# Two layers of a pooling and attention trunk: VectorE instead of GpSimd adds the two branches, and the sums of weights are all made in the first layer

## The chip, the cores and the metric

The kernel runs on one core of a Trainium2 chip. The metric is the time of one execution on the device in microseconds (us). The core's engines run side by side, each through its own queue in order: TensorE (PE, with its weight loads shown as PEld) multiplies matrices, VectorE (DVE), ScalarE (ACT) and GpSimd (POOL) work element by element, and SyncE (SP) starts transfers (DMAs). Engines wait for each other through semaphores. GpSimd starts transfers too.

## The reference, cut to what matters

The model width is 1024, there are 512 tokens and 16 meta tokens ahead of them (528 in all), and two layers. Everything is float32. Per layer:

```
h = rmsnorm(h_res, norm_gain[l])
u_pool, z_pool, c_q, c_kv, k_rope, z_mla, g_pool, g_mla = split(h @ w_in[l])
y_pool = (pool_mix(u_pool, pool_w_group[l], pool_scale[l]) * silu(z_pool)) @ pool_w_up[l]
o_mla  = mla(c_q, c_kv, k_rope, ...)            # 8 heads, causal, low-rank q and kv, QK-norm, rotary
y_mla  = (o_mla * silu(z_mla)) @ mla_w_up[l]
merged = sigmoid(g_pool) * y_pool + sigmoid(g_mla) * y_mla
h_res  = h_res + merged @ w_out[l]
```

`pool_mix` takes causal means over windows of 2, 4, 8 and 16 tokens in four groups of channels, subtracts the token itself and multiplies by a 128x128 matrix per group. The meta tokens are dropped from the output.

## The kernel before

**Tiles.** Channels lie on the 128 partitions, tokens along the free axis. A product of 1024 channels is eight output tiles of 128 channels; each is computed from eight blocks of 128 input channels. Every float32 operand is split into a high part and a rest (`hh`/`hl` for activations, `whi`/`wlo` for weights), and one block of a product is three matmuls (`mm3`, lines 188, 191, 192): high by high, rest by high, high by rest. In the first layer an output tile is made in two segments of 264 tokens; in the last layer in one of 512, since the meta tokens are no longer needed there.

**The stream of weights.** `register` lists all products of both layers in the order in which TensorE does them: latent inputs, `u`, `zp`, `y` (the pooled branch), `qr`/`qn`, `pu` (up-projection of the pooled branch), `zm`, gates, `mu` (up-projection of the attention branch) and `o` (output). `stream` walks the list in chunks of 512 weight columns (256 KB) and has the loads four chunks ahead. `wload` starts the load into one of three buffers `raw` on SP's queue (line 115); ScalarE makes `whi` (line 183) and VectorE `wlo` (line 184), and then the `raw` buffer is free for the next load. A loop in `go` places everything else, such as the attention heads, between steps of the stream; `after(ns, fn)` has a piece of work done when the stream has gone on by a modelled time. A scheduler then sets each engine's order from a modelled timeline.

**Merging the branches (`ev_mu`, lines 1046 to 1054).** `am[m]` holds tile m of the gated pooled branch, in the buffer `xb`; `gms[m]` holds the attention gate, in a `cq` buffer. For each segment of an up-projection tile VectorE computes (gate + 1) times the matmul's result (line 1051), GpSimd adds the pooled branch (line 1052), ScalarE takes the high part `hh` (line 298), and VectorE the rest `hl` (line 299). The output products read these as `hh`/`hl` of block m. After the up-projection `blend` (lines 1086 to 1089) forms further sums of tiles on VectorE for the output products.

**Sums of weights (`weight_sums`).** Some output tiles and gates are computed in pairs with seven smaller products instead of eight, which needs sums of quarters of two weight tiles. They are made by transfers alone, in device memory (`wsum`): a copy on SP's queue (line 351), and an accumulating transfer on GpSimd's queue (line 354). A unit takes four of each; there are two units for each layer's output weights and four for the last layer's pooled gates (`gp`). Each transfer is held back until a matmul that stands some way back in the stream has been done:

```python
def copy(d, src):
    behind(sp.dma_start(d, src[0]), earlier(9000))

def add(d, src):
    behind(gp.dma_start(d, src[1], accum_op=ALU.add), earlier(4000))
```

In the first layer `go` starts them after `qn3`: 16 transfers for the first layer's output weights, one per 3500 modelled ns, then 22 of the 32 for the gates, one per 4000. The other ten are kept in the list `jobs` and placed at the start of the last layer, from `norm_sums` on. The last layer's own output weights are summed during its heads.

**Start of a layer (`norm_sums`).** The rows of inverse norms go out to memory by four small transfers (`ndr`, lines 434 and 435) and come back spread over all partitions (`rinv` and `q`, line 440), all on SP's queue, in which the weight loads stand as well.

Of the kernel before, what the change touches and what calls it, by code (L numbers as in the profile page):

```python
# [23 lines left out]
T = SEQ + NM  # L24
# [15 lines left out]
MT_GP = 16  # L40
# [18 lines left out]
OUT = (3, 4, 5, 6)  # L59
# [13 lines left out]
def trunk(ctx, tc, xT, pos, win, wkr, wqb, wkb, wvb, wgr, wpu, wmu, wout, gains, const, yT):  # L73
    nc = tc.nc
    pe, act, dve, gp, sp = nc.tensor, nc.scalar, nc.vector, nc.gpsimd, nc.sync
# [86 lines left out]
    class Gemm:  # L162
        def __init__(self, name, src, width, evac=None, xs=None, segs=None, body=None, gain=None):
            self.name, self.src, self.width, self.alloc = name, src, width, mmt
            self.evac, self.xs, self.segs, self.body, self.gain = evac, xs, segs, body, gain
            self.spare = self.more = False
# [30 lines left out]
    def earlier(ns):  # L197
        return next((m for c, m in reversed(past) if c <= clk[0] - ns), past[0][1])

    newest = [None]  # L200
    jobs = []
    plan = []
    done = set()

# [57 lines left out]
    def after(ns, fn):  # L262
        pend.append((clk[0] + ns, fn))
        pend.sort(key=lambda e: e[0])
# [9 lines left out]
    def upto(name):  # L274
        while name not in done:
            if not step():
                break
# [19 lines left out]
    def split(hi, lo, src, a, b):  # L297
        act.activation(hi[:, a:b], src, AF.Copy)  # L298
        dve.tensor_sub(lo[:, a:b], src, hi[:, a:b].bitcast(F32))  # L299

    def behind(ins, other):
        tc.add_manual_dep(ins.ins, other.ins.name,
                          mybir.DependencyInfo(mybir.DependencyClass.Sync, mybir.DependencyReason.DATA))
# [38 lines left out]
    def weight_sums(name, w):  # L342
        def made(u, i):
            a, b = w[2 * u], w[2 * u + 1]
            d = wsum[name][u]
            src = {0: (b[:, 0:512], b[:, 512:1024]), 2: (a[:, 0:512], b[:, 0:512]), 1: (a[:, 0:512], d[:, 0, :]),
                   3: (a[:, 512:1024], d[:, 1, :])}
            return d[:, i, :], src[i]
# [7 lines that stand above are left out]
        for u in range(len(w) // 2):  # L356
            for fn, i in ((copy, 0), (copy, 2), (add, 0), (copy, 1), (add, 2), (add, 1), (copy, 3), (add, 3)):
                yield lambda fn=fn, u=u, i=i: fn(*made(u, i))

    class Layer:  # L360
        def __init__(self, l):
            self.l, self.last = l, l == DEPTH - 1
            self.XS = XTOK if self.last else FULL
            self.x0 = NM if self.last else 0
            self.xt = xt if l == 0 else [None] * 8
            self.hs, self.us, self.zps = hbuf, [None] * 4, [None] * 4
            self.cs, self.cqs, self.ys, self.am = [None] * 2, [None] * 6, [None] * 4, [None] * 8
            self.kn, self.qn, self.zms, self.ogs = [None] * 4, [None] * 4, [None] * 4, [None] * 4
            self.qr, self.qf = [None] * 2, [None] * 2
            self.gms, self.mg, self.xr, self.vw = [None] * 8, [None] * 8, [None] * 8, []  # L370
            self.made = [None] * 8
            self.csq, self.xsq = [None] * 2, [None] * 8
            self.sq = []
            self.sums = [None] * 8
            self.f, self.tt, self.part = [None] * 8, [None] * 4, {}
            self.st = self.acc = self.inv = self.cinv = self.kraw = self.kp = None

# [668 lines left out]
        def ev_mu(self, m):  # L1046
            def ev(ps, a, b):
                if a == self.x0:
                    self.mg[m] = self.hs[m]
                t = self.gms[m][:, a:b]  # L1050
                dve.scalar_tensor_tensor(out=t, in0=t, scalar=1.0, in1=ps, op0=ALU.add, op1=ALU.mult)  # L1051
                self.sums[m] = gp.tensor_add(t, t, self.am[m][:, a:b])  # L1052
                split(*self.mg[m], t, a, b)
            return ev

        def ev_o(self, m, nxt):
# [187 lines left out]
        def go(self, nxt):  # L1244
            l = self.l
            up = lambda name: upto((l, name))
# [10 lines left out]
                for k in range(8):  # L1257
                    self.square_x(k)
            self.norm_sums()
            if l == 1:  # L1260
                for i in range(len(jobs)):
                    after(4000 * (i + 1), jobs.pop(0))
            up("u1")
            for m in range(2):
                self.mix(m, self.window(m))
# [6 lines left out]
            up("zp1")  # L1272
            self.mix(3, s3)
            self.k_factors()
            up("qr1")
            for s, (a, b) in enumerate(FULL):
                a0 = max(a, self.x0)
                self.stat(self.acc[:, a0:b], a0, b, C_CQ, self.acc_last)
            up("qn3")
            if l == 0:  # L1280
                jobs.extend(weight_sums("gp", [win[1, MT_GP + m] for m in range(8)]))
                for i, fn in enumerate(weight_sums(0, [wout[0, m] for m in OUT])):
                    after(3500 * (i + 1), fn)
                for i in range(22):
                    after(16 * 3500 + 4000 * (i + 1), jobs.pop(0))
            self.qk_stats()
            if l == 0:
                fill_now(2600)
# [117 lines left out]
```

## Time and profile before

| | |
|---|---|
| median of 3 runs | 793.72 us (793.56 to 794.35) |
| the profiled execution, its own time | 794.64 us |
| its span, first to last instruction | 792.8 us |
| busy share: PE, PEld, DVE, ACT, POOL | 98%, 90%, 76%, 56%, 30% |
| line 1052 on GpSimd, 24 instructions | 28.6 us |
| transfers from start to landing, median | weights (`raw<-win`) 2.8 us; copies for sums 3.5 to 4.0; accumulating ones 5.7 to 6.1 |

TensorE is busy for nearly all of the span, so its short waits are what can be won, and new waits of it are what can be lost. Where a view lists windows, it gives for each stretch its length and each engine's busy time with the number of instructions that fall in it, then the granted TensorE clock (1.00 is full), the DMA engines' busy share and GB/s. Where a view lists waits, it gives the total, the number and the longest. A name such as `mm<-hl,whi` says what is written from what, without buffer numbers; a time of a transfer is from its start on the queue to its landing.

### The profile page before, as it was taken

What the parts mean: (1) busy time and instruction counts of PE and PEld (TensorE: products, weight loads), DVE (VectorE), ACT (ScalarE), POOL (GpSimd) and SP (SyncE); (2) the same over time, 40 slices, a digit from 0 to 9 for tenths busy, and PEclk for the clock granted to TensorE, in tenths of its full rate; (3) what the DMA queues carried; (4) which work ended last, traced back from release to release, by engine and by line L of the source; (5) the groups of instructions that cost most, each with busy time, mean ns of one, the idle gap of its engine ahead of it and who ended that gap; (6) DMA issues with size and microseconds to landing.
All of it is one profiled execution on the core that took longest, in us unless ns stands there. A gap on an engine that the chain in (4) does not pass through costs nothing. (4 is left out here: it accounts for less than half of the span.)

```text
span 792.8 us, 15386 instructions
## 1 busy us (share of the span) xinstructions
PE 778.1 (98%) x5493; PEld 713.7 (90%) x5493; DVE 601.0 (76%) x1321; ACT 443.6 (56%) x1015; POOL 238.5 (30%) x315
## 2 busy tenths in 40 slices
PE   8999999999999999999999999999999999999898
PEld 8999899999999999999997887887788989988687
DVE  5848788447788887689865378775997989975985
ACT  8536656645566565545564256555657766763451
POOL 1034505013443352072100246131026335431601
PEclk9999999999999999999999999999999999999999
DMA  6242343566546546655632754435456666662552
GB/s 241 82 101 92 90 118 101 153 146 159 130 122 142 129 121 136 162 146 176 183 116 74 139 126 122 132 87 175 124 128 147 182 164 169 166 232 82 165 165 80
DMA packets 65196, 109.15 MB, mean 138 GB/s; under 512 B 10448, under 2 KB 16976, under 8 KB 65120
## 3 DMA queue, kind: packets, MB, share of 16 engines
q1 hardware_dynamic: 58096, 93.72, 40.3%
q0 software_dynamic: 6016, 12.62, 9.8%
q10 hardware_dynamic: 1008, 1.84, 0.6%
q8 instruction: 43, 0.70, 0.4%
q14 instruction: 33, 0.27, 0.1%
HBM read 100.18 MB, written 22.62 MB: 155 GB/s over the span
## 5 line engine op out<-in xcount | busy, mean ns | idle before, releaser
L188 PE MATMUL mm<-hh,whi 128*128 128x264 f32 (+2 forms) x1000 | 308.7, 311 | 2.9 <-ACT whi L183 2.8
L191 PE MATMUL mm<-hl,whi 128*128 128x264 f32 (+2 forms) x1000 | 306.9, 308 | 2.3 <-DVE hl L299 2.3
L192 PE MATMUL mm<-hh,wlo 128*128 128x264 f32 (+2 forms) x1000 | 306.4, 309 | 1.0 <-DVE wlo L184 1.0
L184 DVE TENSOR_TENSOR wlo<-raw,whi 128x512 fp32r<-128x512 f32 (+2 forms) x261 | 195.3, 752 | 100.0 <-ACT whi L183 93.6
L183 ACT ACTIVATE whi<-raw 128x512 fp32r<-128x512 f32 (+2 forms) x261 | 156.2, 602 | 142.7 <-PE mm L191 76.5
L188 PEld LDWEIGHTS mm<-hh,whi 128*128 128x128 f32 x1000 | 188.2, 189 | 14.0 <-ACT whi L183 3.5
L191 PEld LDWEIGHTS mm<-hl,whi 128*128 128x128 f32 x1000 | 188.7, 189 | 12.0 <-DVE hl L299 3.2
L192 PEld LDWEIGHTS mm<-hh,wlo 128*128 128x128 f32 x1000 | 187.8, 189 | 10.4 <-DVE wlo L184 2.1
L192 PE MATMUL mm<-cq,wlo 128*128 128x264 f32 (+2 forms) x156 | 48.0, 310 | 0.7 <-DVE wlo L184 0.7
L188 PE MATMUL mm<-cq,whi 128*128 128x264 f32 (+2 forms) x156 | 48.6, 311 | 0.0
L704 POOL TENSOR_TENSOR racc<-racc,tmp 128x264 f32<-128x264 f32 (+1 forms) x15 | 14.3, 952 | 112.2 <-ACT tmp L703 88.1
L191 PE MATMUL mm<-cq,whi 128*128 128x264 f32 (+2 forms) x140 | 43.5, 312 | 0.0
L1052 POOL TENSOR_TENSOR cq<-cq,xb 128x264 f32<-128x264 f32 (+1 forms) x24 | 28.6, 1220 | 46.8 <-DVE cq L1051 46.6
L881 DVE CUSTOM_DVE_ANT_0 S<-S,maskw,nqs 128x288 f32<-128x288 f32 (+4 forms) x80 | 38.2, 496 | 2.6 <-PE S L192 2.4
L188 PE MATMUL mm<-u,whi 128*128 128x264 f32 (+1 forms) x108 | 35.2, 326 | 0.0
L192 PE MATMUL mm<-u,wlo 128*128 128x264 f32 (+1 forms) x108 | 34.8, 322 | 0.0
L299 DVE TENSOR_TENSOR tl<-mm,th 128x512 fp32r<-128x512 f32 (+1 forms) x64 | 29.4, 480 | 7.0 <-ACT th L298 6.0
L354 POOL DMA_DIRECT2D wsum<-wout x8 | 6.8, 848 | 87.8 <-PE mm L192 82.2
L852 POOL TENSOR_TENSOR tmp<-kp,bc 64x528 f32<-64x528 f32 x16 | 24.8, 1550 | 25.8 <-DVE xb L653 9.5
L192 PEld LDWEIGHTS mm<-cq,wlo 128*128 128x128 f32 x156 | 29.4, 188 | 2.6 <-DVE wlo L184 1.1
L928 POOL TENSOR_TENSOR cq<-cq,rs 128x384 f32<-128x384 f32 (+1 forms) x32 | 31.6, 989 | 0.0
L888 ACT ACTIVATE cq<-S,bia 128x400 f32<-128x400 f32 (+2 forms) x48 | 24.5, 515 | 12.1 <-DVE bia L916 7.9
(341 smaller groups left out, 1714.6 us busy)
## 6 DMA issues: line engine op xcount, KB each, us to landing
raw<-win SPq DMA_DIRECT2D x139, 256.0 KB, 2.8
raw<-wout SPq DMA_DIRECT2D x22, 256.0 KB, 3.0
bc<-kdr SPq DMA_DIRECT2D x16, 264.0 KB, 4.6
raw<-wpu SPq DMA_DIRECT2D x16, 256.0 KB, 3.0
wsum<-wout SPq DMA_DIRECT2D x16, 256.0 KB, 3.5
wsumgp<-win SPq DMA_DIRECT2D x16, 256.0 KB, 4.0
raw<-wmu SPq DMA_DIRECT2D x16, 256.0 KB, 2.8
raw<-wsumgp SPq DMA_DIRECT2D x16, 256.0 KB, 3.4
```

What stands on the lines that cost most here:

```text
L183: act.activation(hi[:, :n], raw[:, :n], AF.Copy)
L184: dve.tensor_sub(lo[:, :n], raw[:, :n], hi[:, :n].bitcast(F32))
L188: first = pe.matmul(out, wh, xh, start=start, stop=False, skip_group_check=more)
L191: pe.matmul(out, wh, xl, start=False, stop=False, skip_group_check=more)
L192: newest[0] = pe.matmul(out, wl, xh, start=False, stop=stop, skip_group_check=more)
L299: dve.tensor_sub(lo[:, a:b], src, hi[:, a:b].bitcast(F32))
L704: self.acc_last = gp.tensor_add(self.acc[:, a:b], self.acc[:, a:b], t[:, :b - a])
L852: gp.tensor_mul(kf[r0:r0 + 64, :], self.kp[r0:r0 + 64, :], bc[r0:r0 + 64, :])
L881: dve.tensor_tensor_reduce(out=sv, in0=sv, in1=mask, scale=nqs[:, i, h:h + 1], scalar=3e38, op0=ALU.add, op1=ALU.min, accum_out=bia[:, c:c ...
L888: act.activation(pv, sv, AF.Exp, scale=-1.0, bias=bia[:, i:i + 1], accum_out=rs[:, c:c + 1])
L928: gp.tensor_mul(pt[i][:, NM:], pt[i][:, NM:], rs[:, i:i + 1].to_broadcast([P, n - NM]))
L1052: self.sums[m] = gp.tensor_add(t, t, self.am[m][:, a:b])
```

## The change

GpSimd no longer adds the pooled branch. VectorE adds it, once per tile and over all tokens, when the tile's last segment has come (in the first layer that joins two segments); the split into `hh` and `hl` is then done once over the whole tile too. The sums of weights for the first layer's output and for the last layer's gates are now all 48 started after `y3`, ahead of `qr`, in one row at 4000 modelled ns each. The list `jobs` and its use in the last layer are gone.

```diff
-    jobs = []
...
-            self.sums = [None] * 8
...
                 dve.scalar_tensor_tensor(out=t, in0=t, scalar=1.0, in1=ps, op0=ALU.add, op1=ALU.mult)
-                self.sums[m] = gp.tensor_add(t, t, self.am[m][:, a:b])
-                split(*self.mg[m], t, a, b)
+                if b == T:
+                    t, x0 = self.gms[m], self.x0
+                    dve.tensor_add(t[:, x0:T], t[:, x0:T], self.am[m][:, x0:T])
+                    split(*self.mg[m], t[:, x0:T], x0, T)
             return ev
...
-            if l == 1:
-                for i in range(len(jobs)):
-                    after(4000 * (i + 1), jobs.pop(0))
             up("u1")
...
             self.k_factors()
+            up("y3")
+            if l == 0:
+                sums = [*weight_sums(0, [wout[0, m] for m in OUT]), *weight_sums("gp", [win[1, MT_GP + m] for m in range(8)])]
+                for i, fn in enumerate(sums):
+                    after(4000 * (i + 1), fn)
             up("qr1")
...
             up("qn3")
-            if l == 0:
-                jobs.extend(weight_sums("gp", [win[1, MT_GP + m] for m in range(8)]))
-                for i, fn in enumerate(weight_sums(0, [wout[0, m] for m in OUT])):
-                    after(3500 * (i + 1), fn)
-                for i in range(22):
-                    after(16 * 3500 + 4000 * (i + 1), jobs.pop(0))
             self.qk_stats()
```

Three places show what the scheduler makes of it. In the names, `raw` is a weight buffer, `wsumgp3` a unit of sums for the gates, `ndr` the small transfers of the norms, `cq5` the tile of up-projection 5, and `mm_1946`, `mm_1971`, `mm_1981` the first three output tiles of the last layer.

SP's queue at the start of the last layer, before:

```order
L435 DMA ndr11_118<-ny2_1098_6122 16x1
L351 DMA wsumgp2_125<-win 128x512
L115 DMA raw_1140_6309<-win 128x512
L115 DMA raw_1145_6341<-wkb 128x256
L440 DMA rinv_1100_6141<-ndr10_117 128x528
L440 DMA q1_1101_6142<-ndr11_118 128x528
L115 DMA raw_1149_6375<-win 128x512
L115 DMA raw_1157_6404<-win 128x512
L351 DMA wsumgp3_126<-win 128x512
L115 DMA raw_1162_6437<-wkr 128x256
L351 DMA wsumgp3_126<-win 128x512
```

And after the change:

```order
L433 DMA ndr11_118<-ny2_1098_6108 16x1
L115 DMA raw_1140_6294<-win 128x512
L115 DMA raw_1145_6326<-wkb 128x256
L438 DMA rinv_1100_6127<-ndr10_117 128x528
L438 DMA q1_1101_6128<-ndr11_118 128x528
L115 DMA raw_1149_6359<-win 128x512
L115 DMA raw_1157_6388<-win 128x512
L115 DMA raw_1162_6420<-wkr 128x256
```

The copies have gone from this part of the queue, and the loads follow the norms directly; five copies and five accumulating transfers leave the last layer in all.

VectorE at the end of the last layer's up-projection, before:

```order
L299 TENSOR_TENSOR hl4_15_141<-cq4_1902_9653,hh4_14_140 128x512
L1051 SCALAR_TENSOR_TENSOR cq5_1903_9655<-cq5_1903_9655,mm_1934_9812 128x512
L184 TENSOR_TENSOR wlo_1992_10068<-kh_1990_10065,whi_1991_10067 128x512
L299 TENSOR_TENSOR hl6_19_145<-cq6_1887_9611,hh6_18_144 128x512
L1051 SCALAR_TENSOR_TENSOR cq7_1907_9681<-cq7_1907_9681,mm_1942_9858 128x512
L184 TENSOR_TENSOR wlo_2002_10110<-kl_2000_10107,whi_2001_10109 128x512
L299 TENSOR_TENSOR hl5_17_143<-cq5_1903_9655,hh5_16_142 128x512
L184 TENSOR_TENSOR wlo_1970_9950<-raw_1968_9947,whi_1969_9949 128x512
L299 TENSOR_TENSOR hl7_21_147<-cq7_1907_9681,hh7_20_146 128x512
```

And after the change:

```order
L1049 SCALAR_TENSOR_TENSOR cq7_1907_9657<-cq7_1907_9657,mm_1942_9834 128x512
L184 TENSOR_TENSOR wlo_2002_10086<-kl_2000_10083,whi_2001_10085 128x512
L298 TENSOR_TENSOR hl4_15_141<-cq4_1902_9629,hh4_14_140 128x512
L1052 TENSOR_TENSOR cq5_1903_9631<-cq5_1903_9631,xb_77 128x512
L1052 TENSOR_TENSOR cq7_1907_9657<-cq7_1907_9657,xb_77 128x512
L298 TENSOR_TENSOR hl6_19_145<-cq6_1887_9587,hh6_18_144 128x512
L184 TENSOR_TENSOR wlo_1970_9926<-raw_1968_9923,whi_1969_9925 128x512
L184 TENSOR_TENSOR wlo_1976_9957<-raw_1974_9954,whi_1975_9956 128x512
L298 TENSOR_TENSOR hl5_17_143<-cq5_1903_9631,hh5_16_142 128x512
L298 TENSOR_TENSOR hl7_21_147<-cq7_1907_9657,hh7_20_146 128x512
```

The eight adds now stand among VectorE's own rows: from the first `cq0` (line 1051, now 1049) to `hl7` there were 25 rows, and now there are 34.

TensorE where it first needs `hl5` in the last layer. Before, this is its 29th matmul behind the up-projection's last one:

```order
L192 MATMUL mm_1971_9953<-hh2_10_136,wlo_1949_9901 128x512
L188 MATMUL mm_1971_9953<-hh3_12_138,whi_1948_9900 128x512
L191 MATMUL mm_1971_9953<-hl3_13_139,whi_1948_9900 128x512
L192 MATMUL mm_1971_9953<-hh3_12_138,wlo_1949_9901 128x512
L188 MATMUL mm_1946_9885<-hh5_16_142,whi_1944_9881 128x512
L191 MATMUL mm_1946_9885<-hl5_17_143,whi_1944_9881 128x512
```

After the change it is the 45th:

```order
L188 MATMUL mm_1981_9982<-hh2_10_136,whi_1975_9956 128x512
L191 MATMUL mm_1981_9982<-hl2_11_137,whi_1975_9956 128x512
L192 MATMUL mm_1981_9982<-hh2_10_136,wlo_1976_9957 128x512
L188 MATMUL mm_1981_9982<-hh3_12_138,whi_1975_9956 128x512
L191 MATMUL mm_1981_9982<-hl3_13_139,whi_1975_9956 128x512
L192 MATMUL mm_1981_9982<-hh3_12_138,wlo_1976_9957 128x512
L191 MATMUL mm_1946_9861<-hl5_17_143,whi_1944_9857 128x512
```

The scheduler has put the first half of the third output tile ahead of block 5 of the first.

## The prediction

> **What bounds the kernel now.** I read the page's first part, then TensorE's waits by stretch, then windows around them, and last the timeline and the transfers at these places.
>
> ```profile
> span 792.8 us, 15386 instructions
> PE 778.1 (98%) x5493; PEld 713.7 (90%) x5493; DVE 601.0 (76%) x1321; ACT 443.6 (56%) x1015; POOL 238.5 (30%) x315
> ```
>
> TensorE bounds it: only 14.7 us of 792.8 are idle. No other engine's work counts by itself; what counts is which of TensorE's waits go and which come. Its waits in four stretches (total, number, longest): 20 to 330 us, which is nearly all of the first layer up to the up-projection; 440 to 452; 466 to 476; and 476 to 482 us, the last three at the start of the last layer.
>
> ```profile
> PE o L954 <- DVE tl L299: 0.2, 1, 0.2
> ...
> PE mm L188 <- ACT whi L183: 1.4, 1, 1.4
> ...
> PE mm L192 <- DVE wlo L184: 0.5, 1, 0.5
> ...
> PE mm L188 <- DVE u L545: 0.8, 1, 0.8
> ```
>
> The first layer, with most of the 38 transfers for sums that it makes, has 0.2 us of waits in 310 us; the last layer's start has more in 40. A wait costs more than its row says, since a matmul's own time overlaps the next one's. So I take the cost from windows: the length less the matmuls that begin in it at their steady pitch.
>
> ```profile
> core 0: us, PE busy (x) PEld busy (x) DVE busy (x) ACT busy (x) POOL busy (x), PEclk, DMA share, GB/s
> 446.80:449.50 2.70, 1.07 (x7) 0.66 (x6) 1.01 (x2) 1.62 (x3) 0.88 (x1) 1.00 0.99 267
> 469.10:473.10 4.00, 3.04 (x19) 2.26 (x18) 3.81 (x9) 2.13 (x7) 1.20 (x2) 1.00 0.44 83
> 479.90:482.20 2.30, 1.53 (x9) 1.13 (x8) 2.30 (x4) 0.63 (x1) 2.19 (x3) 1.00 0.62 122
> 361.70:362.50 0.80, 0.57 (x5) 0.36 (x4) 0.60 (x2) 0.58 (x2) 0.18 (x1) 1.00 0.59 225
> 748.10:750.60 2.50, 0.47 (x3) 0.04 (x2) 2.50 (x4) 0.79 (x3) 2.14 (x2) 1.00 0.26 88
> 751.75:755.15 3.40, 3.40 (x10) 2.63 (x9) 3.40 (x10) 0.97 (x2) 0.00 (x0) 0.50 0.69 207
> 386.00:406.00 20.00, 20.00 (x166) 20.00 (x166) 16.24 (x33) 12.87 (x23) 3.25 (x6) 1.00 0.44 142
> ```
>
> The last row gives the pitch of a 264-token matmul: 20.00/166 = 0.12 us; a 512-token one takes 0.23 (below). By that the last layer's start loses 2.70 - 7 x 0.12 = 1.9, then 4.00 - 19 x 0.12 = 1.7, then 2.30 less one short and six long ones (1.5) = 0.8: 4.4 us. The first layer's step from up-projection to output loses 0.80 - 3 x 0.12 = 0.4. The last layer's same step is the dearest: the wait in 748.10 to 750.60, and behind it a stretch with a granted clock of 0.50.
>
> **The change part by part: sums leave the last layer's start.** Starts of transfers on SP's queue and the ScalarE row that took up the late weights come from the timeline, the landings (last column) from the transfers' view, first in the last layer, then at the same place in the first.
>
> ```profile
> 434.74 0.50 SPq L435 DMA_DIRECT2D ndr<-ny  x1
> 435.29 0.51 SPq L351 DMA_DIRECT2D wsumgp<-win  x1
> 447.83 1.09 ACT L183 ACTIVATE whi<-raw 128x512 fp32r<-128x512 f32 x2 [6.71 <-DMA raw<-win]
> ...
> ndr<-ny SPq DMA_DIRECT2D x1, 0.1 KB, 8.7
> wsumgp<-win SPq DMA_DIRECT2D x1, 256.0 KB, 12.1
> ...
> 41.16 0.50 SPq L435 DMA_DIRECT2D ndr<-ny  x1
> 41.76 0.37 SPq L115 DMA_DIRECT2D raw<-win  x1
> ...
> ndr<-ny SPq DMA_DIRECT2D x1, 0.1 KB, 8.9
> raw<-win SPq DMA_DIRECT2D x1, 256.0 KB, 8.7
> ```
>
> In the first layer the last small transfer lands at 41.16 + 8.9 = 50.1 and the weights right behind it at 41.76 + 8.7 = 50.5. In the last layer it lands at 434.74 + 8.7 = 443.4, then the copy for the sums at 435.29 + 12.1 = 447.4, and only then the weights, taken up at 447.83. The copy alone stands between, and costs 4.0 us. Without it the weights land at about 443.8, and TensorE, which runs dry at 446.9, has them: the 1.9 go. For the 1.7 us I compare the loads of 449 to 471 us with those of 52 to 74 us, which are the same kinds in the first layer with no sums beside them:
>
> ```profile
> raw<-win SPq DMA_DIRECT2D x5, 256.0 KB, 5.9
> raw<-wkb SPq DMA_DIRECT2D x3, 128.0 KB, 5.0
> ...
> raw<-win SPq DMA_DIRECT2D x5, 256.0 KB, 3.0
> raw<-wkb SPq DMA_DIRECT2D x3, 128.0 KB, 2.0
> ```
>
> Half the latency is the sums'. I take back 1.4 of 1.7, since two of the small waits there are not for weights, and half of 0.8, whose wait row names VectorE's evacuation of `u`. Five copies and five accumulating transfers leave: -3.7 us, between 0 and -4.4.
>
> **VectorE adds.** GpSimd loses 24 adds; VectorE gains 16 of full width and, in the first layer, 8 wide `hl` take the place of 16 narrow ones; ScalarE has 8 rows fewer. In the last layer, where a tile is one segment:
>
> ```profile
> 729.40 1.29 DVE L1051 SCALAR_TENSOR_TENSOR cq<-cq,mm 128x512 f32<-128x512 f32 x2 [2.88 <-PE mm L192]
> ...
> 741.16 0.68 DVE L299 TENSOR_TENSOR hl<-cq,hh 128x512 fp32r<-128x512 f32 x1
> 741.49 0.40 PE L192 MATMUL mm<-q,wlo 128*128 128x512 f32 x1
> 741.72 0.39 PE L188 MATMUL mm<-hh,whi 128*128 128x512 f32 x1
> 741.76 0.68 DVE L1051 SCALAR_TENSOR_TENSOR cq<-cq,mm 128x512 f32<-128x512 f32 x1
> ...
> 748.14 0.39 PE L188 MATMUL mm<-hh,whi 128*128 128x512 f32 x1
> 748.32 1.64 POOL L1052 TENSOR_TENSOR cq<-cq,xb 128x512 f32<-128x512 f32 x1 [1.22 <-DVE cq L1051]
> 748.77 1.75 DVE L299 TENSOR_TENSOR hl<-cq,hh 128x512 fp32r<-128x512 f32 x1
> 750.57 0.50 PE L191 MATMUL mm<-hl,whi 128*128 128x512 f32 x1 [2.03 <-DVE hl L299]
> 751.04 0.68 DVE L299 TENSOR_TENSOR hl<-cq,hh 128x512 fp32r<-128x512 f32 x1
> ```
>
> An undisturbed VectorE row of 512 takes 0.68 us and the next starts 0.60 later (741.16 to 741.76); beside a GpSimd add the same `hl` took 1.75 and ended just after it. So the add on GpSimd costs VectorE about as much as an add of its own. From 729.40 on, 34 rows at 0.60 put the start of `hl7`, the last, at 729.40 + 33 x 0.60 = 749.2 and that of `hl5`, one row ahead, at 748.6, done at 749.3; before, 25 rows brought `hl5` to 750.5 and `hl7` to 751.7. TensorE also asks later: the 45th matmul behind the up-projection's last, not the 29th, so 16 x 0.23 = 3.7 us later than 748.4, at 752.1. The scheduler's reordering thus leaves 2.8 us to spare where 2.0 were lacking. The nearest need is `hl4`, the 26th: at 741.49 + 26 x 0.23 = 747.5, and VectorE's eighth row from the end, `hl4`, starts at 745.0 and is done at 745.7. What this wait costs now is 750.57 - 748.14 - 0.23 = 2.2 us, and in the clock's stretch eight matmuls began in 3.40 us, where 8 x 0.23 = 1.8 would do: 1.6 more. Together 3.8. VectorE is the next to be late: it stays full in the output stage, and one split of weights there has little room, so I leave 0.5: -3.3 us, between 0 and -3.8.
>
> [...]
>
> In the first layer the adds cost nothing by themselves, as TensorE's tile there takes 24 x 0.12 = 2.9 us and VectorE's three rows of full width and two halves, counted as a fourth, 4 x 0.60 = 2.4. The 0.4 us wait should go: -0.3, between 0 and -0.4.
>
> **What the sums cost in the first layer.** The ten transfers go there, and all start earlier, at `y3` instead of behind `qn3`. From 141 to 165 us they ran at 3500 ns each, denser than any will:
>
> ```profile
> 141.00:165.00 24.00, 24.00 (x208) 22.40 (x208) 10.78 (x31) 12.83 (x32) 1.04 (x1) 1.00 0.58 149
> ...
> SPq L351 <- PE mm L192: 33.8, 20, 4.4
> ```
>
> TensorE was full there, so I cost `qr` and `qn` at nothing; their cover is the three `raw` buffers and four chunks ahead, and if it were gone each load would be late by the 3 us of the comparison above. The other place is the first layer's output, where four copies now stand on SP's queue among loads of output weights and as many accumulating transfers on GpSimd's ahead of the stores of `xb`. Behind a copy that waits for its matmul (33.8 us over 20 waits, 1.7 on average, 4.4 at most) stand weight loads. The bounds are 0, since these loads mostly wait for a `raw` buffer longer than that, and the 4.4 us that five copies and five sums took from the last layer's start, where the buffers are the same. I take 0.8, nearer to nothing by the quiet 20 to 330 us.
>
> **The sum.** -3.7 - 3.3 - 0.3 + 0.8 = -6.5 against this execution's 794.64 us, whose span of 792.8 has 1.8 around it that doesn't change: 788.1. The median of the runs, 793.72, is 0.9 less: 787.2.
>
> **The rivals.**
> First, the waits at the last layer's start stay, because the small `ndr` transfers of 8.7 us make them, not the copies. For: they land late in both layers. Against: the first layer's weights landed 0.4 us behind them. Without that term: 787.2 + 3.7 = 790.9.
> Second, VectorE, with 34 rows where 25 stood, becomes the one that is waited for, and the last layer's step stays as dear. For: it was busy all of 2.50 us in the wait's window. Against: 1.1 us of each `hl` beside GpSimd was waiting. 787.2 + 3.3 = 790.5.
> Third, the clock halves at that place whatever the wait: 787.2 + 1.6 = 788.8.
> Fourth, slower: the copies in the first layer's output hold up SP's queue. A chunk there is twelve matmuls, 12 x 0.12 = 1.4 us, so a late load is soon felt. Four copies at 3.05 us, between the average and the longest wait, with nothing covering them, cost 12.2 in place of 0.8: 798.6. It decides once the four cost more than the 7.3 us won, 1.8 each, just above the average wait; at the average itself the result is 793.2, no change.
>
> **How the numbers follow.** The forecast has 0.54, the first and second rival 0.12 each, the third 0.06, the fourth 0.16, of which 0.05 at no change. Within 0.2%, 1.6 us, a measurement of this kernel can't tell a difference. So faster 0.84, same 0.05, slower 0.11. The range goes from all that can be won, 793.72 - 4.4 - 3.8 - 0.4 = 785.1, to 791.2, just beyond the first rival and the sum with the first layer's cost at its bound of 4.4 (790.8).
>
> **What would show it.** Right: no wait of TensorE over 0.5 us between 440 and 452, and loads there that land in about 3 us; no clock of 0.50 behind the last up-projection, and every `hl` at 0.68 us. Loads of output weights in the first layer that stay under 5 us show the fourth rival wrong; TensorE waiting there for `whi` or `wlo` by microseconds would make the prediction wrong, as would a wait for `hl` in the last layer as long as now.

## The result, and the profile after

| | before | changed |
|---|---|---|
| median of 6 runs | 793.73 us (793.17 to 795.92) | 789.46 us (787.08 to 790.89) |
| ratio of the runs | | 0.994, 95% interval 0.9919 to 0.9961 |
| the profiled execution, its span | 794.64, 792.8 us | 790.13, 788.4 us |

The change wins 0.6%: 4.8 us by the ratio (3.1 to 6.4 by its interval) and 4.3 between the medians, where 6.5 were forecast. First the head of the page of the changed kernel:

```profile
span 788.4 us, 15369 instructions
...
PE 776.1 (98%) x5493; PEld 713.6 (91%) x5493; DVE 592.9 (75%) x1329; ACT 442.5 (56%) x1007; POOL 212.4 (27%) x291
```

TensorE does the same 5493 matmuls. So I count them through in both traces and take the time from the k-th to the l-th (a matmul or two stand in another order there, which shifts a bound by tenths). In us, with the bounds as times of the trace of before:

| stretch | before | changed | difference |
|---|---|---|---|
| 1 to 19: start | 17.9 | 18.6 | +0.7 |
| 271 to 328: end of the first layer's heads and gates | 57.5 | 56.8 | -0.7 |
| 328 to 345: first layer's up-projection begins | 16.4 | 19.6 | +3.2 |
| 345 to 378: its end, and the step to the output | 33.5 | 33.4 | -0.1 |
| 432 to 491: the last layer's start | 59.0 | 54.2 | -4.8 |
| 736 to 789: last layer's step to the output, and the output | 53.2 | 49.8 | -3.4 |
| all the rest | 550.5 | 551.1 | +0.6 |

Both gains are there. One new cost of 3.2 us has come, at a place that the prediction does not name. The waits of TensorE in the changed kernel, from 440 to 482 us, from 320 to 340 and from 735 to 785; between them, second, the kernel before from 320 to 340:

```profile
PE mm L188 <- DVE u L543: 0.3, 1, 0.3
...
PE mm L188 <- ACT q L298: 0.2, 1, 0.2
...
PE mm L188 <- ACT q L297: 1.9, 1, 1.9
...
PE mm L188 <- ACT whi L183: 0.9, 1, 0.9
PE S L188 <- ACT whi L183: 0.4, 1, 0.4
```

The last layer's start has lost its waits but for 0.3 us, and the 2.0 us for `hl` are gone. VectorE's rows in the last layer's up-projection, grouped by shape (number, then total in us and mean in ns), before (722 to 752 us) and changed (722 to 750 us):

```profile
L299 DVE TENSOR_TENSOR hl<-cq,hh 128x512 fp32r<-128x512 f32 x8 | 9.8, 1226 | 0.0
L184 DVE TENSOR_TENSOR wlo<-raw,whi 128x512 fp32r<-128x512 f32 x9 | 9.0, 997 | 0.7 <-ACT whi L183 0.7
L1051 DVE SCALAR_TENSOR_TENSOR cq<-cq,mm 128x512 f32<-128x512 f32 x8 | 5.3, 677 | 2.9 <-PE mm L192 2.9
```

```profile
L184 DVE TENSOR_TENSOR wlo<-raw,whi 128x512 fp32r<-128x512 f32 x8 | 5.4, 683 | 0.3 <-ACT whi L183 0.3
L298 DVE TENSOR_TENSOR hl<-cq,hh 128x512 fp32r<-128x512 f32 x8 | 5.4, 682 | 0.0
L1052 DVE TENSOR_TENSOR cq<-cq,xb 128x512 f32<-128x512 f32 x8 | 5.4, 681 | 0.0
L1049 DVE SCALAR_TENSOR_TENSOR cq<-cq,mm 128x512 f32<-128x512 f32 x8 | 5.3, 678 | 2.9 <-PE mm L192 2.9
```

The eight adds now take 5.4 us of VectorE; `hl` alone gives 4.4 back, and `wlo`, at 683 ns in place of 997, some 2.5 more. Of the three kinds of before, the two with both inputs in SBUF had been slowed (`hl` 1226 ns against 682, `wlo` 997 against 683). The row that reads a matmul's result took 677 ns on average before and 678 after, and the three of its eight that ran beside a GpSimd add took no longer than the others (0.67 to 0.68 us).

The new wait, in the transfers begun from 325 to 329 us (number, KB each, median us from start to landing), before and changed, and then in the windows of both (328 to 345 us, then 335.5 to 339 of the changed kernel):

```profile
raw<-wmu SPq DMA_DIRECT2D x3, 256.0 KB, 2.8
wsumgp<-win POOLq DMA_DIRECT2D x1, 256.0 KB, 6.7
```

```profile
raw<-wmu SPq DMA_DIRECT2D x3, 256.0 KB, 4.4
wsumgp<-win POOLq DMA_DIRECT2D x1, 256.0 KB, 5.1
wsumgp<-wsumgp POOLq DMA_DIRECT2D x1, 256.0 KB, 5.5
```

```profile
328.00:345.00 17.00, 16.75 (x137) 16.50 (x137) 12.79 (x33) 8.30 (x22) 5.56 (x6) 1.00 0.55 148
...
328.00:345.00 17.00, 15.08 (x110) 14.82 (x110) 9.61 (x28) 6.35 (x17) 1.65 (x2) 0.90 0.62 162
335.50:339.00 3.50, 3.50 (x19) 3.50 (x18) 2.21 (x8) 1.27 (x4) 0.00 (x0) 0.51 0.65 154
```

Two accumulating transfers for sums now run beside two loads of up-projection weights (begun at 327.24 and 327.84 us), which take 4.4 us. The timeline shows how that reaches TensorE, first two rows of the kernel before, then the changed one:

```profile
330.94 1.29 DVE L184 TENSOR_TENSOR wlo<-raw,whi 128x512 fp32r<-128x512 f32 x2 [0.94 <-ACT whi L183]
...
332.27 0.23 DVE L1015 COPY mo<-mm 128x64 f32<-128x64 f32 x1
...
331.72 1.16 ACT L183 ACTIVATE whi<-raw 128x512 fp32r<-128x512 f32 x2 [2.67 <-DMA raw<-wmu]
...
332.39 1.29 DVE L184 TENSOR_TENSOR wlo<-raw,whi 128x512 fp32r<-128x512 f32 x2 [2.62 <-ACT whi L183]
...
333.71 0.23 DVE L1013 COPY mo<-mm 128x64 f32<-128x64 f32 x1
...
334.64 0.31 ACT L297 ACTIVATE q<-tmp 128x16 fp32r<-128x16 f32 x2
```

TensorE does not want these weights yet. It waits for `q`, the split attention output, which starts with the copy `mo` on VectorE; and VectorE, in its fixed order, first stands 2.6 us (0.9 before) before a split of the late weights. Behind the wait the granted clock is 0.50 for 3.41 us (335.52 to 338.94), as it was before in the last layer (751.75 to 755.16).

### The profile page after: what moved, and what is told of

Its sections match the earlier page's. It is cut to its first block, busy times and chain, and to the rows that moved or that the text cites. A ratio compares the mean times of both kernels' runs of the same rounds, so it can differ in the third digit from the quotient of the medians.

```text
span 788.4 us, 15369 instructions
## 1 busy us (share of the span) xinstructions
PE 776.1 (98%) x5493; PEld 713.6 (91%) x5493; DVE 592.9 (75%) x1329; ACT 442.5 (56%) x1007; POOL 212.4 (27%) x291
## 4 chain that ended last, share of the span: by engine, by line
PE 89%; DMA 4%; DVE 3%; issue 2%; ACT 2%; POOL 0%; ACTq 0%; DVEq 0%; POOLq 0%
PE mm L188 26%; PE mm L192 26%; PE mm L191 25%; PE mm L946 2%; PE S L191 2%; PE S L188 2%; PE S L192 2%; DMA raw<-win 1%; DVE wlo L184 1%; PE o L952 1%; PE o L951 1%; DMA raw<-wout 1%; PE S L500 1%; ACT whi L183 1%; DMA xb<-xT 1%
## 5 line engine op out<-in xcount | busy, mean ns | idle before, releaser
L184 DVE TENSOR_TENSOR wlo<-raw,whi 128x512 fp32r<-128x512 f32 (+2 forms) x261 | 188.6, 727 | 98.5 <-ACT whi L183 91.6
L188 PE MATMUL mm<-cq,whi 128*128 128x264 f32 (+2 forms) x156 | 48.6, 312 | 0.9 <-ACT whi L183 0.9
L188 PE MATMUL mm<-q,whi 128*128 128x264 f32 (+1 forms) x96 | 30.5, 329 | 1.9 <-ACT q L297 1.9
L188 PEld LDWEIGHTS mm<-cq,whi 128*128 128x128 f32 x156 | 29.4, 188 | 2.6 <-ACT whi L183 1.1
```

Source lines behind the costliest of these rows:

```text
L184: dve.tensor_sub(lo[:, :n], raw[:, :n], hi[:, :n].bitcast(F32))
L188: first = pe.matmul(out, wh, xh, start=start, stop=False, skip_group_check=more)
```

## The experiments

Ratios are to the kernel before, run on the same chip beside it (medians there 794.27 to 795.12 us, and 793.73 for the first row of the changed kernel). The stretches, from the matmul count of each kernel's trace:

| kernel | ratio, 95% interval | 328-345 | 345-378 | 432-491 | 736-789 |
|---|---|---|---|---|---|
| before | | 16.4 | 33.5 | 59.0 | 53.2 |
| changed | 0.994 (0.9919 to 0.9961) | 19.6 | 33.4 | 54.2 | 49.8 |
| `changed_again` | 0.9924 (0.9897 to 0.9951) | 19.5 | 33.7 | 53.6 | 50.5 |
| `sums_moved_only` | 0.9953 (0.9934 to 0.9971) | 19.5 | 33.4 | 53.6 | 53.2 |
| `vector_add_only` | 0.9973 (0.9958 to 0.9987) | 16.4 | 32.9 | 58.3 | 50.4 |
| `two_sums_later` | 0.9909 (0.988 to 0.9938) | 16.2 | 33.5 | 54.3 | 50.5 |
| `sums_late_pause` | 0.995 (0.9931 to 0.9968) | 16.5 | 35.4 | 53.8 | 50.2 |
| `sums_every_3000` | 0.9918 (0.9894 to 0.9941) | 16.3 | 32.9 | 53.7 | 49.8 |
| `idle_adds_beside` | 1.0004 (0.9987 to 1.0021) | 16.2 | 35.8 | 54.2 | 54.3 |
| `no_pooled_add` | 0.9911 (0.9882 to 0.9941) | 16.2 | 33.0 | 53.6 | 48.6 |
| `stores_by_gpsimd` | 0.9903 (0.9876 to 0.993) | 16.3 | 32.9 | 53.6 | 49.6 |
| `one_copy_behind` | 0.9917 (0.989 to 0.9944) | 16.3 | 32.9 | 55.1 | 49.6 |
| `five_copies` | 0.9913 (0.988 to 0.9946) | 16.2 | 32.9 | 54.6 | 49.5 |
| `five_adds` | 0.9902 (0.9875 to 0.9929) | 16.1 | 32.9 | 57.4 | 49.6 |

Intervals of some 0.5% cannot part kernels that differ by a microsecond; what does is the stretch in which a kernel was edited, where the others agree to some tenths. A stretch is of one execution, though, and has the halved clock in it or not.

**Each part alone.** The first against the changed kernel, the second against the one before:

```diff
-                if b == T:
-                    t, x0 = self.gms[m], self.x0
-                    dve.tensor_add(t[:, x0:T], t[:, x0:T], self.am[m][:, x0:T])
-                    split(*self.mg[m], t[:, x0:T], x0, T)
+                gp.tensor_add(t, t, self.am[m][:, a:b])
+                split(*self.mg[m], t, a, b)
```

> The sums of weights are all started after y3, but GpSimd still adds the pooled branch, segment by segment. Theory: the two parts of the change are independent of each other. Then the last layer's start is shorter by the 4.9 us that the profile after shows, the first layer's up-projection has the new wait of 1.9 us for q (with the halved clock behind it in part of the runs: 1.4 to 3.1 us together), and the last layer's step from up-projection to output keeps its wait of 2.0 us for hl and its halved clock: 790 to 792 us. Rival: the new wait comes from VectorE's new rows, not from the transfers; then it is absent here and the time is about 789.

```diff
-                self.sums[m] = gp.tensor_add(t, t, self.am[m][:, a:b])
-                split(*self.mg[m], t, a, b)
+                if b == T:
+                    t, x0 = self.gms[m], self.x0
+                    dve.tensor_add(t[:, x0:T], t[:, x0:T], self.am[m][:, x0:T])
+                    split(*self.mg[m], t[:, x0:T], x0, T)
```

> VectorE adds the pooled branch, and the sums stay where they were, with ten transfers in the last layer. Theory: only the last step from up-projection to output changes, by 2.9 to 3.8 us, and the first layer's by up to 0.5; no wait over 0.5 us for q in the first layer's up-projection; the waits at the last layer's start stay at 1.4 us and more: 789.7 to 790.6 us. Rival (the new wait comes from VectorE's rows): a wait of about 1.9 us for q in the first layer's up-projection, 791.5 to 793.

Measured: 791.09 and 792.08 us. Each part's large effects stay where they were: the parts are nearly independent. With the sums moved alone the new wait for `q` (1.8 us) is there and the `hl` wait of 2.0 stays. With VectorE's add alone the `q` wait is 0.2 us, as before, and the last stretch falls to 50.4. By the ratios the sums give 3.7 us (2.3 to 5.2) and the add 2.1 (1.0 to 3.3); the second came out below the 2.9 to 3.8 expected of the last step alone, though its interval reaches 3.3. Its trace shows why its last stretch is not better still, a new wait in the output stage:

```profile
PE mm L188 <- ACT whi L183: 1.3, 1, 1.3
PE S L188 <- ACT whi L183: 0.4, 1, 0.4
```

**The new wait in the first layer.** Three ways to shift the two accumulating transfers against the loads; each line replaces the loop's `after(...)`, where the changed kernel has `4000 * (i + 1)`:

```diff
+                    after(3000 * (i + 1), fn)                                      # sums_every_3000
+                    after(4000 * (i + 1) + (12000 if i >= 36 else 0), fn)          # sums_late_pause
+                    after(4000 * (i + 1) + (8000 if i in (36, 37) else 0), fn)     # two_sums_later
```

> The changed kernel with the 48 transfers for sums one per 3000 modelled ns instead of 4000, so that all have landed ahead of the first layer's up-projection. Theory: the 1.9 us wait there is made by two accumulating transfers that run beside two loads of up-projection weights (4.4 us each where they took 2.7 before); without them no wait over 0.5 us and no halved clock: 786 to 787.5 us, with every run at a full clock. Rival: the denser row of transfers makes loads late earlier in the first layer, with waits over 0.5 us between 116 and 320 us: 789 or more.

> The changed kernel with the last twelve transfers for sums put off by 12000 modelled ns more, so that none runs beside the loads of the first layer's up-projection and more run in its output stage. Theory (collision of loads with accumulating transfers): the wait for q falls to 0.5 us or less, the time to 786 to 788 us. Rival (the fourth of the prediction): the transfers in the output stage hold up loads there; a wait over 1 us for whi or wlo between 340 and 400 us, and 789 or more.

> The changed kernel (sums at 4000) in which only two of the 48 transfers are held back 8000 modelled ns longer: the two accumulating ones that ran beside the loads of up-projection weights at 325.6 and 328.2 us. The order on every queue is unchanged. Theory (these two make the loads late, and through them the meta tokens' rows on VectorE and the matmul of q): the stretch from 328 to 345 us falls from 19.6 us to 16.5, with no wait over 0.5 us, and the time by 1.4 to 3.1 us against the changed kernel of the same chip. Rival (the copies on SP's queue or something else make the loads late): the wait stays at 1 us or more.

> The changed kernel once more, as the partner of the run before it on the same chip, and to see in how many executions the clock is halved behind the wait of 1.9 us. From the six executions so far: about half of them at a mean clock of 0.998 or less, these some 2.6 us longer than the others; 0.994 of the time before.

The third settles it. It changes no order on any queue, only what two transfers wait for, and they start 2.7 and 0.7 us later (327.96 and 328.53 us, against 325.25 and 327.80 in `changed_again`). Its transfers begun from 325 to 329 us, and its window from 328 to 345:

```profile
raw<-wmu SPq DMA_DIRECT2D x3, 256.0 KB, 2.6
wsumgp<-win POOLq DMA_DIRECT2D x1, 256.0 KB, 5.5
wsumgp<-wsumgp POOLq DMA_DIRECT2D x1, 256.0 KB, 7.0
...
328.00:345.00 17.00, 16.96 (x139) 16.70 (x138) 13.02 (x33) 6.82 (x17) 2.44 (x3) 1.00 0.84 196
```

The loads land in 2.6 us, the wait is gone, and 786.80 us (786.38 to 788.31) stand beside the 788.91 (787.28 to 789.94) of the changed kernel on the same chip: 2.1 us less, inside the 1.4 to 3.1 expected. The transfers still run beside the loads; what has changed is that the loads have begun first. What moved from 327.3 to 329.5 us, on GpSimd's queue (q0, here the accumulating transfers) and SP's (q1, here the loads; packets, MB, share of the engines), first in the changed kernel, then in `two_sums_later`:

```profile
q0 software_dynamic: 96, 0.19, 83.5%
q1 hardware_dynamic: 11, 0.01, 1.1%
...
q1 hardware_dynamic: 208, 0.39, 66.7%
```

Where an accumulating transfer began 1.6 us ahead of the first load, hardly a packet of the loads moved before 329.5 us; where it began 0.9 us behind that load, the loads went first, and in the kernel before, where it began behind both (at 328.39 us), they took 2.7 us. The two transfers were moved together, so which of them does it is not shown. Of the partner's seven executions only two had a mean clock of 0.998 or less; they took 789.5 us on average, the others 788.2. That is 1.3 us and not the 2.6 expected.

`sums_every_3000` also loses the wait, at 786.34 us (785.05 to 789.85). Its denser transfers are not always free: two of the later kernels with this spacing, `stores_by_gpsimd` and `one_copy_behind`, show a new wait of 1.2 and 1.5 us at 154 us, where ScalarE stands before late `raw<-wpu` (for 3.85 us in `one_copy_behind`, against 1.97 in `sums_every_3000`). `sums_late_pause` loses the `q` wait as well, but not the time (789.95 us), since it moves twelve transfers into the output stage. Of its waits from 340 to 400 us the first is new, and the second was 0.3 us in the changed kernel:

```profile
PE S L188 <- ACT whi L183: 1.1, 1, 1.1
PE S L188 <- ACT sv L1142: 0.8, 1, 0.8
```

So the fourth rival's cost exists (35.4 us in that stretch against 33.4), and is met only when more transfers are put there than the changed kernel has. Whether the copies or the accumulating transfers make it is not parted here.

**Is it GpSimd's row itself that slows VectorE?** From here on the sums are at 3000, and the base is `sums_every_3000`.

```diff
-                dve.scalar_tensor_tensor(out=t, in0=t, scalar=1.0, in1=ps, op0=ALU.add, op1=ALU.mult)
+                made = dve.scalar_tensor_tensor(out=t, in0=t, scalar=1.0, in1=ps, op0=ALU.add, op1=ALU.mult)
+                behind(gp.tensor_add(tmp()[:, :b - a], self.am[m][:, a:b], self.am[m][:, a:b]), made)
```

> The sums at 3000, and 24 additions on GpSimd of the old size (the pooled branch to itself, into a spare tile) come back, each held until VectorE's row of line 1049 for that segment has been done; nobody reads them, and VectorE's and TensorE's order is the same as in the kernel with the sums at 3000 (786.3 us). Theory (GpSimd's row holds up VectorE's by itself): rows of 512 on VectorE beside them take about 1.75 us instead of 0.68; eight such rows in the last layer make VectorE some 8 us later, of which 2.8 were to spare: a wait for hl or for a weight split of 2 us or more behind the last up-projection, 788.5 to 793 us. Rival (what counted was that the result came by way of GpSimd, and where hl5 stood): no wait over 0.5 us there, 785.5 to 787.1.

Measured: 795.06 us, ratio 1.0004, more than the 793 at which the expectation ended. Twenty-four GpSimd rows that nobody reads take back the whole 0.8% of the base. VectorE's rows in the last up-projection (722 to 752 us), TensorE's waits there, and the window behind:

```profile
L184 DVE TENSOR_TENSOR wlo<-raw,whi 128x512 fp32r<-128x512 f32 x8 | 7.6, 962 | 0.0
L1053 DVE TENSOR_TENSOR cq<-cq,xb 128x512 f32<-128x512 f32 x8 | 7.3, 922 | 0.0
L1049 DVE SCALAR_TENSOR_TENSOR cq<-cq,mm 128x512 f32<-128x512 f32 x8 | 5.3, 678 | 2.9 <-PE mm L192 2.9
L298 DVE TENSOR_TENSOR hl<-cq,hh 128x512 fp32r<-128x512 f32 x6 | 4.9, 820 | 0.0
...
PE mm L191 <- DVE hl L298: 2.0, 1, 2.0
PE mm L192 <- DVE wlo L184: 0.3, 1, 0.3
...
749.00:752.40 3.40, 3.05 (x9) 1.75 (x8) 3.40 (x6) 1.23 (x2) 1.39 (x3) 0.53 0.81 241
```

A wait of 2.0 us for `hl` is back with the halved clock behind it, though no data passes through GpSimd. It is now for `hl4`, which TensorE needs ahead of `hl5` in this order. VectorE's last `hl` starts 25.1 us after its first row of line 1049, where the base and the changed kernel have 20.2: eight GpSimd rows cost VectorE 4.9 us, about 0.6 each, and not the 8 us expected. The first layer's step pays 2.9 us too (35.8 against 32.9). As in the kernel before, the rows with both inputs in SBUF were the slower ones (means of 820 to 962 ns), and the row that reads a matmul's result was not (678).

**What VectorE's adds cost, and the wait that came.** `no_pooled_add` leaves the pooled branch out of the merged output, and so gives another result; `stores_by_gpsimd` takes the stores of output tiles off the queue of loads.

```diff
-                    dve.tensor_add(t[:, x0:T], t[:, x0:T], self.am[m][:, x0:T])
```

> The sums at 3000, and the pooled branch is left out of the merged output: nobody adds it, so VectorE has 8 rows fewer in the last layer's up-projection and 8 in the first's. It asks what VectorE's adds cost by themselves. Theory (VectorE is the next to be late, through the splits of weights behind which loads wait): the two waits for whi of 0.9 us in the last layer's output stage fall below 0.4 each, and the time by 1.0 to 2.0 us from 786.3: 784.3 to 785.3. Rival: the adds are hidden and those waits come from the queue of loads itself: 785.8 to 786.8.

```diff
-                    sp.dma_start(yT[:, m, a - NM:b - NM], xn[:, a:b])
+                    gp.dma_start(yT[:, m, a - NM:b - NM], xn[:, a:b])
```

> The sums at 3000, and the five last stores of the output tiles that stand on SP's queue among loads of output weights (line 1070) go on GpSimd's queue; VectorE's and TensorE's order is unchanged. Theory (loads of weights stand behind stores that wait for VectorE): the waits for whi of 0.9 us in the last layer's output stage fall below 0.4, 785 to 786 us. Rival (the loads wait for a free buffer, hence for VectorE's split, whatever stands ahead of them): the waits stay, 786 to 787.

Without the add the trace has no wait at all from 735 to 785 us, and the last stretch is 1.2 us shorter (48.6). With the stores moved the waits stay at 0.7 and 0.4. So VectorE's load makes them, not the queue: the loads of `raw<-wsum` start once VectorE has split what lay in the buffers (in the changed kernel two splits end at 757.20 and 757.80 us, and the loads start at 757.23 and 757.83). In the whole time neither shows: 788.62 (786.64 to 789.28) and 788.45 us (785.77 to 788.94), within the spread of the base by their ratios; both are above the times that were expected, which ended at 787.

**What made the last layer's start late.** One copy, five copies, or five accumulating transfers come back there, at the old places, into a memory that nobody reads:

```diff
             self.norm_sums()
+            if l == 1:                                                   # one_copy_behind: the first of these alone
+                for i in (0, 2, 3, 5, 8):                                # five_copies
+                    after(4000 * (i + 1), lambda: behind(sp.dma_start(dead, win[1, MT_GP, :, 0:512]), earlier(9000)))
+                for i in (1, 4, 6, 7, 9):                                # five_adds, without the copies
+                    after(4000 * (i + 1), lambda: behind(gp.dma_start(dead, win[1, MT_GP, :, 0:512], accum_op=ALU.add), earlier(4000)))
```

> The sums at 3000, and a single copy of 256 KB on SP's queue right behind the last small transfer of the norms in the last layer, into a memory that nobody reads; every other order is unchanged. Theory (the copy alone stands between): the weights behind it land some 4 us later and TensorE waits for whi there as before, 1.4 us in the waits and 1.9 in time: 787.7 to 788.7 us. Rival (only the crowd of ten transfers made the loads late): weights later by less than 2 us, no wait over 0.5 us, 785.5 to 787.1.

> The sums at 3000, and five copies of 256 KB on SP's queue at the start of the last layer, at the places where the kernel before has its five, into a memory that nobody reads; no accumulating transfers there. With none the stretch from 432 to 491 us took 53.7 us, with one copy 55.1, before 59.0. Theory (the copies on SP's queue carry the loss): 58 to 59 us in that stretch. Rival (the accumulating transfers carry it as well): 55 to 56.5 us.

> The sums at 3000, and five accumulating transfers of 256 KB on GpSimd's queue at the start of the last layer, at the places where the kernel before has its five, into a memory that nobody reads (one copy in the first layer fills it); no copies there. With none the stretch from 432 to 491 us took 53.7 us, with five copies 54.6, before 59.0. Theory now (the accumulating transfers carry the loss, by holding up GpSimd's queue or the loads beside them): 57 to 59 us. Rival (only copies and accumulating transfers together do it, or those of the kernel before are late for another reason): 54 to 56 us.

Measured: 789.27, 787.38 and 787.13 us; the stretch takes 55.1, 54.6 and 57.4 us, with none 53.7. Five copies came out below both of their ranges, and the single copy's time above both of its. None of the three ratios (0.9902 to 0.9917) is above the base's 0.9918, so the whole time shows none of these costs; what follows is read from one execution of each. TensorE's waits from 436 to 492 us, in that order:

```profile
PE mm L188 <- DVE u L544: 1.2, 1, 1.2
...
PE mm L192 <- DVE wlo L184: 0.2, 1, 0.2
...
PE mm L188 <- DVE u L544: 1.9, 1, 1.9
```

The single copy landed 1.1 us behind the last `ndr` transfer, and the weights 0.65 behind it, so TensorE did not wait for `whi`. With five accumulating transfers the stretch is 3.7 us longer: a wait of 1.9 us for `u`, and a lower clock behind it, 0.69 on average from 452.5 to 458 us, which is 1.7 more. The wait comes about as in the first layer. The weights land behind `q` on SP's queue, and VectorE stands before their split ahead of its row for `u`:

```profile
451.58 0.69 DVE L184 TENSOR_TENSOR wlo<-raw,whi 128x512 fp32r<-128x512 f32 x1 [4.26 <-ACT whi L183]
```

But the load of `q` landed 2.1 us later than in the base, counted from the start of the last `ndr` transfer, and 1.0 of that is this `ndr` itself (10.6 us against 9.6), which had been under way for 9.9 us when the first accumulating transfer began. So how much of the 3.7 the accumulating transfers make is not shown. The two differences together are 4.6 of the 5.3 us between 53.7 and 59.0, but not in the same places. The 1.7 us that the kernel before lost from 469 to 473 and the 0.8 at 480 came back in none of the three. They may need copies and accumulating transfers together; that pair was not tried with idle data. Two rows bear on it, both of the kernel before: GpSimd's waits from 436 to 492 us, and VectorE's rows of line 535 from 468 to 490 us, below which stands the same row in the changed kernel.

```profile
POOL wsumgp L354 <- DMA wsumgp<-win: 5.5, 1, 5.5
...
L535 DVE TENSOR_TENSOR tmp<-tmp,ts 128x264 f32<-128x264 f32 x2 | 3.6, 1791 | 0.0
...
L533 DVE TENSOR_TENSOR tmp<-tmp,ts 128x264 f32<-128x264 f32 x2 | 1.8, 894 | 0.0
```

GpSimd stood 5.5 us before an accumulating transfer that waited for its copy, until 448.08 us, with its own rows queued behind; and at 473.83 and 477.25 us, beside GpSimd rows, VectorE's two rows of line 535 took 0.97 and 2.61 us, on average twice as long as in the changed kernel. That this is the cause is argued, not shown.

## Why the prediction was right or wrong

**The sums leave the last layer's start: -3.7, measured -4.8** (59.0 to 54.2), and -5.4 in `changed_again` and `sums_moved_only`, beyond its bound of -4.4. The comparison of landings was right; the transfers of the changed kernel from 449 to 471 us:

```profile
raw<-win SPq DMA_DIRECT2D x5, 256.0 KB, 2.7
raw<-wkb SPq DMA_DIRECT2D x3, 128.0 KB, 1.9
```

They took 5.9 and 5.0 us before. The step that failed is "The copy alone stands between, and costs 4.0 us": one copy alone cost 1.4 us in the stretch and made no wait for weights, and in `vector_add_only`, with the copy at its place, TensorE ran past that point without a wait. One trace had been read as a fixed cost. What the ten transfers cost together there is shown (58.3 in `vector_add_only` against 54.3 and less without them); how it divides among them stays open. The first rival (the small `ndr` transfers make the waits) fell: they still took 8.1 and 8.2 us, and the waits are gone.

**VectorE adds, last layer: -3.3, measured -3.4.** The reading that a GpSimd add costs VectorE about as much as an add of its own is borne out by `idle_adds_beside` (0.6 us each, where a row of its own takes 0.68 and the next starts 0.60 later), and the second rival fell with it. From the first `cq0` to the start of `hl7` the prediction had 33 x 0.60 = 19.8 us; it took 20.2. Every `hl` took 0.68 us, and no halved stretch stands behind the up-projection, as said. VectorE was next to be late, as said: 1.3 us of waits for `whi` where 0.5 was left for it. Nothing is lost by that in the sum because the stretch of before held more than the 3.8 I had counted: against the trace of `no_pooled_add`, which has no wait there (48.6), it was 4.6 us longer. The 1.6 us for the clock were too much for a mean: of 64 executions of the kernel before, 35 had a mean clock of 0.998 or less, with a median of 795.55 us against 793.76 for the others. So that term is worth 1.8 us in half of the executions, about 1.0 in all. This may be why `vector_add_only` gave 2.1 us by its ratio and 2.8 in its last stretch; the ratio's interval holds both. The third rival (the clock halves whatever the wait) fell: in `vector_add_only` one of twelve executions had a mean clock of 0.998 or less.

**First layer's step to the output: -0.3, measured -0.1,** being -0.6 for the add (32.9 in `vector_add_only`) and +0.5 with a new wait of 0.3 us for `sv`, a row of ScalarE, at the end of the stretch. `changed_again` and `two_sums_later` have that wait too. `vector_add_only`, where fewer transfers for sums run there, doesn't have it, and neither does `sums_moved_only` (33.4), which keeps the old wait of 0.2 us for `hl`. So this half microsecond comes with both parts together; why is not shown.

**The sums' cost in the first layer: +0.8, measured about +3.0** (+3.2, +0.5, and -0.7 ahead of them). This is the term that was mis-sized, and it made the gain 4.5 instead of 6.5 us between the two profiled executions. The bound of 4.4 held it. The step that failed is where I looked: at `qr` and `qn`, where TensorE was full, and at the output, "The other place is the first layer's output". Between them lies the begin of the up-projection, whose own row, a wait for `q` of 0.2 us, said that it had nothing to spare. And the price of a late load was taken as its own lateness, while here a load 1.7 us late (landed at 331.64 us against 330.20, with TensorE 0.2 us earlier in its work) cost a wait longer by 1.7, by way of VectorE's order, and nearly as much again by the clock (0.50 for 3.41 us).

The fourth rival named the right kind of cost (transfers for sums hold up loads in the first layer) with the wrong carrier, the copies on SP's queue, and the wrong place. Of the loads of output weights two did take over 5 us in the changed kernel (7.5 and 6.7; their median was 3.3), but TensorE waited 0.3 us at most there.

With that one collision taken away the forecast's sum comes out: `two_sums_later` has a ratio of 0.9909 and `sums_every_3000` of 0.9918, where 787.2 over 793.72 us is 0.9918. In part that is luck: in `two_sums_later` the last layer's start gained 4.7 us, 1.0 more than forecast, and the last layer's step 2.7, 0.6 less.

## What to carry to other kernels

When background transfers are moved, look for the place with the least slack that they will newly run beside, and not only at the place they leave and the place that is full of work: a shift of two transfers by 0.7 and 2.7 us decided 2 us here, and the loads were late only in the traces where a transfer had begun ahead of them (4.4 us and, in `changed_again`, 4.2, against 2.8 before and 2.6 in `two_sums_later`). Price a late load by everything that stands behind its consumer in that engine's order. And an elementwise row on GpSimd was not free here, though GpSimd was busy for only 30% of the span: beside VectorE rows with two inputs in SBUF it cost VectorE about 0.6 us (`idle_adds_beside`), where doing the row there takes 0.68.

## What was not expected of the hardware

Behind a wait of 1.8 to 2.0 us the granted clock is 0.50 for 3.41 us in the traces of the kernel before and the changed one, and lowered in those of `changed_again`, `idle_adds_beside` and `five_adds` (0.54, 0.53 and 0.69 on average over 3.5, 3.4 and 5.5 us). But that comes only in a third to a little over half of the executions. Outside the profiled execution this is counted by the mean granted clock: one such stretch in 790 us makes it 1 - 0.5 x 3.41 / 790 = 0.998. That or less was the mean in 35 of 64 executions of the kernel before, 6 of 12 of `sums_moved_only` and of `idle_adds_beside`, 5 of 13 of the changed kernel and 2 of 6 of `five_adds`. `sums_every_3000`, `two_sums_later`, `stores_by_gpsimd` and `five_copies`, with no such wait in their traces, had none in 24. The length alone does not settle it: `sums_late_pause` had it in 5 of 7, with waits of 1.1 and 0.8 us less than 2 us apart, and `no_pooled_add` in 2 of 4 with none over 1.1 in its trace; in neither trace itself did the clock halve between the first matmul and the last. What decides in which executions it comes is not shown.

With an accumulating transfer begun 1.6 us ahead of the first of two loads of the same size, 11 packets of the loads moved in 2.2 us, and 208 with the order of the starts turned round. Whether it is a worse neighbour than a copy is less sure: five of them at the last layer's start stand in a stretch of 57.4 us and five copies in one of 54.6, but 1.7 us of that is the halved clock and up to 1.0 may be a slower `ndr`, and the whole times, 787.13 and 787.38 us, don't differ.
